# Hybrid decoder trunk on one core: low parts of 170 weight slabs kept in DRAM between the two halves of the tokens

## The chip, the core and the metric

The kernel runs on one core of a Trainium2 chip. The metric is the device time of one execution in microseconds (us); lower is better. The core has five engines that run their own in-order queues: PE (TensorE, matrix products; its weight loads are shown apart as PEld), DVE (VectorE), ACT (ScalarE), POOL (GpSimd) and SP (SyncE, which here only issues DMAs). DMAs issued by any of them are carried out by 16 DMA engines.

## The reference

A decoder of two layers over 1024 tokens of width 1024, all in float32. Each layer adds three things to the residual h: a mixer of four groups of heads, a cross-attention to 256 memory tokens, and a gated feed-forward of width 2816.

```python
for l in range(DEPTH):                       # DEPTH = 2
    proj = rms_norm(h, norm_mix[l]) @ w_in[l]
    ret_p, rw_p, ssm_p, dsa_p = split_cols(proj, GROUP_COLS)
    ...                                      # retention, RWKV-7, Mamba-2, sparse attention
    h = h + concat([o_ret, o_rw, o_ssm, o_dsa]) @ w_out[l]
    h = h + cross_attention(rms_norm(h, norm_cross[l]), memn, wq, wk, wv, wo)
    h = h + conv_glu(rms_norm(h, norm_ffn[l]), w_up, conv_w, conv_b, w_down)
return rms_norm(h, norm_final)
```

## The kernel before

Everything is held feature-major, and the tokens are worked through in two halves of 512 (`hf` 0 and 1). A large product keeps the accuracy of float32 by splitting both operands into a high part that PE's faster format holds exactly and a low part, the rest. `mm3` (L263) then issues three products for each 128 x 128 block of weights: high by high, high by low, and low by high.

Weights come in **slabs**: 128 partitions by up to 1024 columns, 512 KB. `slab` (L268) makes one. It takes a raw buffer (`wraw`, three of them in pool `wr`), queues its load on SP (L272), copies the high part on ACT into one of two `whi` buffers (L254) and subtracts on DVE for the low part into one of two `wlo` buffers (L258). The raw buffer is free again when the subtraction has read it; `whi` and `wlo` are free when the slab's products are done. A slab of 1024 columns has 24 products of 512 tokens. In the two passes of the out-projection slabs have 640 and 384 columns (15 and 9 products), in the last product of the feed-forward 512 or 640.

The same slab is needed once for each half of the tokens, and before the change it is loaded, copied and subtracted anew each time: 644 slabs in all.

The stages of the main work follow one another in the order that `schedule` (L1829) writes out: the in-projection `proj` (P, 27 slabs a half) and what comes behind the mixers, `outer` (O, 124 slabs a half: out-projection, cross-attention, feed-forward; 8 of them are keys and values, and the last O loads 8 slabs twice). With (layer, half) in brackets and the start of each stage's slabs in the trace:

- P(0,0) from 0 us, together with the first keys and values of the memory tokens
- P(0,1) from about 200 us, beside the rest of the memory tokens
- O(0,0) from about 520 us
- P(1,0) from about 1240 us
- O(0,1) from about 1440 us
- P(1,1) from about 2085 us
- O(1,0) from about 2260 us
- O(1,1) from about 2960 us to the end at 3517.8 us

Beside the main work run two chains of mixer steps (`left`, `right`): many small operations on DVE and ACT with small products on PE, and many DMAs on SP. `paced` (L1790) deals their steps out among those of the main work. A scheduler then orders the instructions of each engine by priority and by its own estimate of when each can run; `urgent` (L391) sets the slabs' steps ahead. Each engine then runs its queue in that order. By about 960 us, 1900 us and 2560 us most of the mixer work of a half is done.

```python
    def mm3(self, out, wh, wl, xh, xl, start=True, stop=True):
        self.mm(out, wh, xh, start, False)
        self.mm(out, wh, xl, False, False)
        self.mm(out, wl, xh, False, stop)
```

Of the kernel before, what the change touches and what calls it, by code (L numbers as in the profile page):

```python
# [9 lines left out]
F32 = mybir.dt.float32  # L10
# [21 lines left out]
MP = 8 * 16 * 129  # words from one 128 x 128 matrix to the next, so that diagonal blocks lie evenly  # L32

# ---------------------------------------------------------------- host layout
GROUPS = [4, 4, 4, 5, 5]
MO_ORDER = [2, 3, 6, 7, 4, 5, 0, 1]  # tiles of the mixers' outputs as they are used
MO_SPLIT = 5
# how far ahead of their place in the program the steps go that the main products wait for
URGENT = 3000
# steps of the in-projection of the first half before the norm of the memory tokens; products of the memory tokens ahead  # L40
# of the in-projection of the second half
PRE, AHEAD = 7, 2
RATE = 100, 100  # of the two chains of mixers against the main work
# [31 lines left out]
J = {"rw": 0, "ds": 8, "rt": 12, "ss": 16}  # first tiles of the in-projection's parts  # L75
# [18 lines left out]
def _consts():  # L94
# [33 lines left out]
    # within a chunk of 64: s < t, s <= t twice, and behind the diagonal blocks of 16  # L128
# [86 lines left out]
# ---------------------------------------------------------------- device  # L215
# head e of a pair, chunk c; partitions of the head's features, of the chunk, and of the chunk where those of e = 1
# have changed places
# [3 lines left out]
class Slab:  # L221
    """hi and lo parts, indexed as one [128, 2, ...] tile"""
# [8 lines left out]
class K:  # L231
    def __init__(self, ctx, tc, a, out, dbg=None):
# [7 lines left out]
        self.wr = pool("wr", 3)  # L240
        self.ws = pool("ws", 2)
# [9 lines left out]
    # ---- helpers  # L251
    def hilo(self, hi, lo, src, lo_eng=None):
        """hi + lo == src exactly, both representable as float32r."""
        self.nc.scalar.copy(hi, src)  # L254
        self.lo(lo, src, hi, lo_eng)
# [12 lines left out]
    def slab(self, src, n=1024):  # L268
        with self.urgent():
            raw = self.wr.tile([128, 1024], F32, name="wraw", tag="wraw")  # L270
            with self.tc.issue_after(self.first.ins) if 0 < len(self.loads) < 4 else nullcontext():
                self.loads.append(self.nc.sync.dma_start(raw[:, :n], src))  # L272
            hi = self.ws.tile([128, 1024], F32R, name="whi", tag="whi")
            lo = self.ws.tile([128, 1024], F32R, name="wlo", tag="wlo")
            self.hilo(hi[:, :n], lo[:, :n], raw[:, :n])
        return Slab(hi, lo)

    def after(self, n):
        """Queues loads behind that of slab n."""
        return self.tc.issue_after(self.loads[n].ins)  # L280
# [4 lines left out]
    def bc(self, ap, n):  # L285
        """[P, 1] -> [P, n] with step 0."""
        return ap.to_broadcast([ap.shape[0], n])

    def rsq(self, pool, src, n, scale, eps, name, bufs=None):
        """(src * scale + eps) ** -0.5 for a [128, n] tile of a few columns."""  # L290
# [10 lines left out]
    # ---- constants  # L301
    def setup(self):
# [11 lines left out]
        # the tables of ScalarE are loaded before the first data are there  # L314
# [40 lines left out]
    # ---- RMSNorm of a feature-major half: hi/lo tiles  # L355
    def sq_acc(self, acc, x, k, eng=None):
        """acc (+)= x * x for tile k of KC; the last addition is the one that is waited for"""
# [9 lines left out]
    def rstd(self, acc, n, nfeat, side=False):  # L367
        """(sum of acc over partitions / nfeat + eps) ** -0.5, token-major"""
# [7 lines left out]
    def rstd_bc(self, r, n):  # L376
        """r on every partition, tokens along the columns"""
# [5 lines left out]
    def gained(self, x, gname, l, k, dst=None):  # L383
        """hi/lo of x times the norm's gain; 1 / rms follows behind the product"""
# [9 lines left out]
    # ---- in-projection of one half  # L394
# [10 lines left out]
    def proj(self, l, hf):  # L405
# [26 lines left out]
        for item in order:  # L432
# [6 lines left out]
            for j in js:  # L439
                w = self.slab(self.a["win"][l, J[name] + j])  # L440
# [4 lines left out]
                # 1 / rms comes in behind the first products  # L445
# [21 lines left out]
    def proj_tok(self, l, hn, r, dst):  # L467
        pss = [(self.pa if t < 2 else self.pt).tile([128, 512], F32, name="ptok", tag="acc")
               for t in range(4)]
        for k0, kn in ((0, 3), (3, 3), (6, 2)):  # L470
            w = self.slab(self.a["wtok"][l, :, k0 * NTOK:(k0 + kn) * NTOK], kn * NTOK)
# [11 lines left out]
    # ---- keys and values of the memory tokens  # L483
# [54 lines left out]
    # ---- out-projection, cross-attention and ConvGLU of one half  # L538
# [9 lines left out]
    def dense(self, l, w, xs, hs, acc, norm):  # L548
        for ks in (range(MO_SPLIT), range(MO_SPLIT, KC)):
            for o in range(8):  # L550
                s = self.slab(self.a[w][l, o, :, ks[0] * 128:(ks[-1] + 1) * 128], len(ks) * 128)
# [43 lines left out]
    def cross(self, l, hn, acc, hs, gain):  # L595
# [9 lines left out]
        def query(h, i):  # L605
            s = self.slab(self.a["wq"][l, 2 * h + i])
# [62 lines left out]
        def out(hp, xo, os):  # L669
            for o in os:  # L670
                s = self.slab(self.a["wo2"][l, hp, o])
# [51 lines left out]
    def ffn(self, l, hf, hn, hs, acc, norm):  # L723
        nc = self.nc
        rb = None  # 1 / rms comes in behind the products
# [6 lines left out]
        def up(f):  # L732
            nonlocal rb
            pss = []
            for i in range(2):
                s = self.slab(self.a["wup"][l, 2 * f + i])
# [37 lines left out]
        for gi, g in enumerate(groups):  # L774
# [11 lines left out]
            # at the very end by halves of the tokens, so that the output of one is scaled beside the other's products  # L786
            parts = [slice(0, TH // 2), slice(TH // 2, TH)] if last and self.own else [slice(0, TH)]
            fin = iter(())
            for cs in parts:
                w = cs.stop - cs.start  # L790
                for o in range(0, 8, 2):
                    # the last tile's products come last in a pair
                    pair = []
                    for o2 in range(2):
                        s = self.slab(self.a["wdn"][l, o + o2, :, g[0] * 128:(g[0] + n) * 128], n * 128)
# [34 lines left out]
    # ---- RWKV-7: elementwise parts by quarters, then blocks of 128 tokens with two chunks of 64  # L830
# [39 lines left out]
    def rw_shift(self, dst, raw, l, hf, c0, tiles):  # L870
        """tiles of the projection with the mix of each token and the one before it"""
# [29 lines left out]
    def rw_pre(self, l, hf, qr, p):  # L901
# [20 lines left out]
        # k (1 + (a - 1) k_a) with a = (1 + ta) / 2  # L922
# [844 lines left out]
    def pool(self, name, bufs, side):  # L1767
        return self.tc.tile_pool(name=name, bufs=bufs, side=side, reuse_waits="tile")
# [96 lines left out]
```

## Time and profile before

| | |
|---|---|
| time, median of 3 runs | 3524.32 us (3523.21 to 3525.83) |
| profiled execution, first to last instruction (span) | 3517.8 us |
| busy: PE, PEld, DVE, ACT, POOL | 96%, 79%, 73%, 49%, 12% of the span |
| low-part subtractions on DVE (L258) | 644, 668.4 us |
| high-part copies on ACT (L254) | 644, 566.9 us |
| moved by DMA | 460.84 MB, mean 131 GB/s |

The profile gives the span of the profiled execution and no other time of its own; the median of the runs lies 6.5 us above it. Products overlap in PE's pipeline, so that one is shown with 0.39 us where the next follows 0.227 us later; PE counts as idle only where no product is under way.

### The profile page before, as it was taken

The page shows a single profiled execution, that of the slowest core. Times are in us where ns is not written, and L with a number is a line of the kernel's source. Part 1 is how long each engine was busy: PE and PEld are TensorE (multiplying, and loading weights), DVE is VectorE, ACT ScalarE, POOL GpSimd, SP SyncE. Part 2 cuts the span into 40 slices and gives each one's busy share as a digit, 9 for nine tenths or more (in the row PEclk, how much of TensorE's full clock was granted, in tenths as well). Part 3 has the DMA queues.
Part 4 walks back from the last instruction along what each step waited for, and adds up shares of the span by engine and source line. Part 5 has one row for each costly group of instructions (what it writes and reads, how often), then busy time and mean ns, then how long its engine had stood idle before and what let it go on. Part 6 is the DMA issues. An engine that isn't in the chain of part 4 may idle for free.

```text
span 3517.8 us, 55280 instructions
## 1 busy us (share of the span) xinstructions
PE 3375.9 (96%) x20256; PEld 2769.4 (79%) x20256; DVE 2578.5 (73%) x5225; ACT 1732.3 (49%) x3298; POOL 412.8 (12%) x449
## 2 busy tenths in 40 slices
PE   8999998999899999999999999999899999999998
PEld 6788886777688877777888887777688888788887
DVE  5885778898879877976886555787888776565555
ACT  4454654588346543544643343378446543443333
POOL 1100002110111111000211010010111112111001
PEclk9999999999999999999999999999999999999999
DMA  8665456432233356433243336532243334222233
GB/s 267 207 196 159 142 195 193 133 98 86 82 112 93 104 193 223 149 110 102 92 130 102 107 120 204 191 116 77 78 130 98 112 102 153 88 93 91 96 102 114
DMA packets 318920, 460.84 MB, mean 131 GB/s; under 512 B 75192, under 2 KB 200504, under 8 KB 318648
## 3 DMA queue, kind: packets, MB, share of 16 engines
q1 hardware_dynamic: 279592, 400.93, 36.1%
q10 hardware_dynamic: 39056, 56.38, 4.6%
q8 instruction: 159, 2.61, 0.3%
q14 instruction: 113, 0.93, 0.1%
HBM read 377.96 MB, written 79.23 MB: 130 GB/s over the span
## 4 chain that ended last, share of the span: by engine, by line
PE 67%; DVE 14%; DMA 7%; ACT 6%; issue 5%; SPq 1%; POOL 0%; ACTq 0%; DVEq 0%; POOLq 0%
PE pacc L261 54%; DVE wlo L258 3%; ACT d_P L1654 3%; DMA d_P<-ds 2%; DVE hn L388 1%; DVE d_P L1630 1%; ACT whi L254 1%; PE dov L261 1%; DVE h L542 1%; PE lg L261 1%; PE dlg L261 1%; PE dtp L1731 1%; PE po L261 1%; DMA d_Q<-in_tab_dram 1%; DMA r_N<-nd 1%
## 5 line engine op out<-in xcount | busy, mean ns | idle before, releaser
L261 PE MATMUL pacc<-hn,whi 128*128 128x512 f32 x5376 | 1725.0, 399 | 31.8 <-ACT hn L254 8.5
L261 PEld LDWEIGHTS pacc<-hn,whi 128*128 128x128 f32 x5376 | 1011.3, 190 | 254.4 <-DVE hn L388 13.2
L261 PE MATMUL pacc<-hn,wlo 128*128 128x512 f32 x2688 | 1071.3, 399 | 33.8 <-DVE wlo L258 33.2
L254 ACT CAST whi<-wraw 128x1024 fp32r<-128x1024 f32 (+5 forms) x644 | 566.9, 882 | 748.5 <-PE pacc L261 591.9
L258 DVE TENSOR_TENSOR wlo<-wraw,whi 128x1024 fp32r<-128x1024 f32 (+5 forms) x644 | 668.4, 1039 | 99.3 <-ACT whi L254 79.0
L261 PE MATMUL pacc<-act,whi 128*128 128x512 f32 (+1 forms) x2256 | 659.4, 375 | 5.1 <-ACT whi L254 4.1
L261 PEld LDWEIGHTS pacc<-hn,wlo 128*128 128x128 f32 x2688 | 511.3, 190 | 155.5 <-DVE wlo L258 49.6
L261 PEld LDWEIGHTS pacc<-act,whi 128*128 128x128 f32 x2256 | 408.5, 189 | 81.1 <-ACT whi L254 8.9
L261 PE MATMUL pacc<-act,wlo 128*128 128x512 f32 (+1 forms) x1128 | 421.6, 377 | 6.8 <-DVE wlo L258 6.5
L542 DVE TENSOR_TENSOR h<-pacc,h 128x512 f32<-128x512 f32 (+1 forms) x296 | 198.1, 672 | 167.6 <-PE pacc L261 166.6
L1654 ACT ACTIVATE d_P<-d_SC,d_cand 128x384 bf16<-128x384 f32 (+3 forms) x248 | 219.1, 884 | 81.1 <-DVE d_cand L1649 66.8
L261 PEld LDWEIGHTS pacc<-act,wlo 128*128 128x128 f32 x1128 | 213.1, 189 | 47.7 <-DVE wlo L258 11.0
L365 POOL TENSOR_TENSOR acc<-acc,sq 128x512 f32<-128x512 f32 (+1 forms) x78 | 107.9, 1383 | 607.5 <-ACT sq L364 601.0
L766 POOL TENSOR_TENSOR cv<-cv,acc 128x512 f32<-128x512 f32 x88 | 125.7, 1429 | 101.4 <-ACT th L765 101.2
L1630 DVE TENSOR_SCALAR_CACHE_REDUCE d_P<-d_SC,d_cand 128x512 bf16<-128x512 f32 (+4 forms) x144 | 135.7, 942 | 2.6
L767 DVE SCALAR_TENSOR_TENSOR cv<-th,cv 128x512 f32<-128x512 f32 x88 | 60.4, 687 | 86.9 <-POOL cv L766 86.9
L765 ACT ACTIVATE th<-cv 128x512 f32<-128x512 f32 x88 | 55.5, 631 | 122.2 <-DVE cv L762 121.7
L254 ACT CAST act<-cv 128x512 fp32r<-128x512 f32 x88 | 54.6, 621 | 121.3 <-DVE cv L769 117.7
L754 DVE TENSOR_TENSOR gs<-pacc,acc 128x512 f32<-128x512 f32 x88 | 60.5, 688 | 71.4 <-PE pacc L261 68.4
L421 DVE TENSOR_TENSOR pev<-pacc,rb 128x512 f32<-128x512 f32 x96 | 65.4, 685 | 42.5 <-PE pacc L261 39.3
L388 DVE SCALAR_TENSOR_TENSOR hn<-h,vec,hn 128x512 fp32r<-128x512 f32 x96 | 90.8, 952 | 3.9 <-ACT hn L387 3.5
L387 ACT ACTIVATE hn<-h,vec 128x512 fp32r<-128x512 f32 x96 | 68.4, 720 | 50.9 <-DVE h L542 49.1
(392 smaller groups left out, 4584.0 us busy)
## 6 DMA issues: line engine op xcount, KB each, us to landing
wraw<-in_wup_dram SPq DMA_DIRECT2D x176, 512.0 KB, 3.3
wraw<-in_win_dram SPq DMA_DIRECT2D x96, 512.0 KB, 3.9
wraw<-in_wdn_dram SPq DMA_DIRECT2D x96, 256.0 KB, 2.6
wraw<-in_wdn_dram SPq DMA_DIRECT2D x72, 320.0 KB, 2.9
wraw<-in_wq_dram SPq DMA_DIRECT2D x32, 512.0 KB, 3.3
wraw<-in_wo_dram SPq DMA_DIRECT2D x32, 512.0 KB, 3.2
r_IN<-sp SPq DMA_DIRECT2D x32, 320.0 KB, 3.8
wraw<-in_wout_dram SPq DMA_DIRECT2D x32, 320.0 KB, 2.7
```

What stands on the lines that cost most here:

```text
L254: self.nc.scalar.copy(hi, src)
L258: (eng or self.nc.vector).tensor_tensor(out=lo, in0=src, in1=hi.bitcast(F32), op=OP.subtract)
L261: self.nc.tensor.matmul(out, lhsT=lhsT, rhs=rhs, start=start, stop=stop)
L365: (eng or (nc.vector if k == KC - 1 else nc.gpsimd)).tensor_tensor(out=acc, in0=acc, in1=s[:, :n], op=OP.add)
L387: self.nc.scalar.mul(hl[:, 0, :], x, g)
L388: self.nc.vector.scalar_tensor_tensor(hl[:, 1, :], x, g, hl[:, 0, :].bitcast(F32), op0=OP.mult, op1=OP.subtract)
L421: nc.vector.tensor_tensor(out=e, in0=ps, in1=rb, op=OP.mult)
L542: self.nc.vector.tensor_tensor(out=h, in0=ps, in1=h, op=OP.add)
L754: nc.vector.tensor_tensor(out=gs[:, 2:], in0=pss[0], in1=rb, op=OP.mult)
L766: nc.gpsimd.tensor_tensor(out=c, in0=c, in1=rb, op=OP.mult)
L1630: ts(junk[:, :n], SC[big[i]], c, None, op0=op, op1=OP.add, accum_out=dst[:, i:i + 1])
L1654: nc.scalar.activation(junka[:, :n], SC[big[i]], AF.Sign, bias=c, accum_out=cnt[:, i:i + 1])
```

## The change

- Of each half-0 slab of the in-projection of both layers (27 + 27) and of `outer` of layer 0 (116: not the keys and values) the low part is also stored to DRAM after the subtraction, by a DMA on SP outside of `urgent`.
- When half 1 comes to the same slab, the raw weights are loaded and the high part copied as before, but the low part is loaded from DRAM by a second DMA on SP. DVE has no subtraction for it. That is 170 slabs: those of P(0,1), O(0,1) and P(1,1).
- `wraw` goes from three buffers to two, `wlo` from two to three, `whi` keeps two; the memory taken is the same.
- `outer` of layer 1 and the slabs of the memory tokens, keys and values do as before, with the new number of buffers.

The diff, without the lines that only take comments away:

```diff
-        self.wr = pool("wr", 3)
-        self.ws = pool("ws", 2)
+        self.wr = pool("wr", 2)
+        self.ws = pool("ws", 3)
+        self.kept = {}
...
-    def slab(self, src, n=1024):
+    def slab(self, src, n=1024, key=None):
+        nc = self.nc
         with self.urgent():
             raw = self.wr.tile([128, 1024], F32, name="wraw", tag="wraw")
+            hi = self.ws.tile([128, 1024], F32R, name="whi", tag="whi", bufs=2)
+            lo = self.ws.tile([128, 1024], F32R, name="wlo", tag="wlo", bufs=3)
             with self.tc.issue_after(self.first.ins) if 0 < len(self.loads) < 4 else nullcontext():
-                self.loads.append(self.nc.sync.dma_start(raw[:, :n], src))
-            hi = self.ws.tile([128, 1024], F32R, name="whi", tag="whi")
-            lo = self.ws.tile([128, 1024], F32R, name="wlo", tag="wlo")
-            self.hilo(hi[:, :n], lo[:, :n], raw[:, :n])
+                self.loads.append(nc.sync.dma_start(raw[:, :n], src))
+            nc.scalar.copy(hi[:, :n], raw[:, :n])
+            if key in self.kept:
+                nc.sync.dma_start(lo[:, :n].bitcast(F32), self.kept[key])
+            else:
+                self.lo(lo[:, :n], raw[:, :n], hi[:, :n])
+        if key is not None and key not in self.kept:
+            self.kept[key] = self.dram("_".join(map(str, ("lo",) + key)), [128, n])
+            nc.sync.dma_start(self.kept[key], lo[:, :n].bitcast(F32))
         return Slab(hi, lo)

+    def key(self, l, *at):
+        return (l,) + at if self.keep[at[0]] > l else None
...
-                w = self.slab(self.a["win"][l, J[name] + j])
+                w = self.slab(self.a["win"][l, J[name] + j], key=self.key(l, "in", J[name] + j))
...
-                s = self.slab(self.a["wup"][l, 2 * f + i])
+                s = self.slab(self.a["wup"][l, 2 * f + i], key=self.key(l, "out", "up", 2 * f + i))
...
+        self.keep = {"in": 2, "out": 1}
```

The other calls of `slab` in `proj_tok`, `dense`, `cross` and `ffn` get their keys in the same way.

## Rows read from the trace of the kernel before

**Rows 1.** The page: span, and PE's busy time, share and instructions.

```profile
span 3517.8 us, 55280 instructions
PE 3375.9 (96%) x20256; PEld 2769.4 (79%) x20256; DVE 2578.5 (73%) x5225; ACT 1732.3 (49%) x3298; POOL 412.8 (12%) x449
```

**Rows 2.** The page: shares of the chain that ended last, by engine.

```profile
PE 67%; DVE 14%; DMA 7%; ACT 6%; issue 5%; SPq 1%; POOL 0%; ACTq 0%; DVEq 0%; POOLq 0%
```

**Rows 3.** The chain in order of time (start, us): its longest piece, in O(1,1).

```profile
3152.51 320.78 PE pacc L261 x1415
```

**Rows 4.** Stretch, length; busy PE, PEld, DVE, ACT, POOL; granted clock, DMA share, GB/s.

```profile
0.00:200.00 200.00, 183.98 (x929) 149.66 (x930) 145.10 (x341) 97.46 (x190) 31.09 (x41) 0.99 0.69 228
200.00:520.00 320.00, 313.49 (x2746) 268.24 (x2744) 228.34 (x569) 157.95 (x338) 7.29 (x15) 0.99 0.55 173
520.00:960.00 440.00, 399.49 (x2707) 314.08 (x2708) 376.45 (x787) 273.50 (x544) 62.06 (x56) 0.97 0.39 119
1240.00:1440.00 200.00, 191.55 (x984) 157.12 (x983) 152.97 (x354) 92.24 (x187) 25.29 (x32) 0.99 0.59 194
1440.00:2085.00 645.00, 626.77 (x3884) 510.59 (x3883) 459.39 (x941) 295.61 (x577) 72.19 (x77) 0.99 0.36 111
2085.00:2260.00 175.00, 171.56 (x843) 139.91 (x842) 107.63 (x193) 65.34 (x114) 22.12 (x17) 1.00 0.56 186
2260.00:2560.00 300.00, 269.99 (x2109) 210.38 (x2108) 244.39 (x539) 200.25 (x403) 26.26 (x24) 0.94 0.34 107
```

**Rows 5.** Groups by line and shape: copies and subtractions (busy us, mean ns, idle before).

```profile
L258 DVE TENSOR_TENSOR wlo<-wraw,whi 128x1024 fp32r<-128x1024 f32 x368 | 457.3, 1243 | 76.0 <-ACT whi L254 56.6 <-PE rbc L261 16.9 <-PE dtp L1731 0.3
L254 ACT CAST whi<-wraw 128x1024 fp32r<-128x1024 f32 x368 | 385.5, 1048 | 449.7 <-PE pacc L261 336.3 <-issue 56.9 <-PE lg L261 11.6
L258 DVE TENSOR_TENSOR wlo<-wraw,whi 128x512 fp32r<-128x512 f32 x128 | 88.4, 691 | 10.9 <-ACT whi L254 10.8
L258 DVE TENSOR_TENSOR wlo<-wraw,whi 128x640 fp32r<-128x640 f32 x104 | 87.7, 846 | 9.4 <-ACT whi L254 8.8
L258 DVE TENSOR_TENSOR wlo<-wraw,whi 128x384 fp32r<-128x384 f32 x32 | 21.5, 671 | 0.0
```

**Rows 6.** Waits of PE (us, times, longest) in 200 to 520, P(0,1).

```profile
PE pacc L261 <- DVE wlo L258: 0.7, 1, 0.7
```

**Rows 7.** Waits of PE in 1440 to 2085 us, O(0,1).

```profile
PE g L261 <- DVE r_Z L1057: 4.2, 1, 4.2
...
PE pacc L261 <- DVE wlo L258: 2.6, 3, 1.2
```

**Rows 8.** Waits of PE in 2085 to 2260 us, P(1,1).

```profile
PE pacc L261 <- DVE wlo L258: 2.1, 1, 2.1
```

**Rows 9.** Waits of PE in 520 to 960 us, O(0,0).

```profile
PE pacc L261 <- DVE wlo L258: 15.2, 15, 2.6
```

**Rows 10.** Waits of PE in 2260 to 2560 us, O(1,0).

```profile
PE pacc L261 <- DVE wlo L258: 10.5, 5, 5.9
```

**Rows 11.** Waits of SP's queue, whole span.

```profile
SPq L272 <- DVE wlo L258: 1588.9, 417, 14.8
```

**Rows 12.** DMA issues: KB each, median us to landing.

```profile
wraw<-in_wup_dram SPq DMA_DIRECT2D x176, 512.0 KB, 3.3
...
sp<-r_o SPq DMA_DIRECT2D x16, 512.0 KB, 3.9
...
wraw<-in_wout_dram SPq DMA_DIRECT2D x32, 192.0 KB, 2.5
```

**Rows 13.** Busy time by stretch, five us of P(0,0), columns as in rows 4.

```profile
80.00:85.00 5.00, 5.00 (x35) 5.00 (x34) 0.92 (x2) 2.19 (x4) 1.06 (x1) 1.00 1.05 400
```

**Rows 14.** ACT in order of time (start, us), slabs of 384 columns in O(1,1).

```profile
2995.56 0.52 ACT L254 CAST whi<-wraw 128x384 fp32r<-128x384 f32 x1 [2.88 <-PE pacc L261]
...
2999.70 0.50 ACT L254 CAST whi<-wraw 128x384 fp32r<-128x384 f32 x1
```

**Rows 15.** DVE in order of time, the subtraction of the first of these.

```profile
2996.39 0.55 DVE L258 TENSOR_TENSOR wlo<-wraw,whi 128x384 fp32r<-128x384 f32 x1
```

More of the change, by code (lines that the diff above doesn't have):

```diff
@@ L470, in proj_tok @@
         for k0, kn in ((0, 3), (3, 3), (6, 2)):
-            w = self.slab(self.a["wtok"][l, :, k0 * NTOK:(k0 + kn) * NTOK], kn * NTOK)
+            w = self.slab(self.a["wtok"][l, :, k0 * NTOK:(k0 + kn) * NTOK], kn * NTOK, self.key(l, "in", "tok", k0))
             for t in range(4):
@@ L550, in dense @@
             for o in range(8):
-                s = self.slab(self.a[w][l, o, :, ks[0] * 128:(ks[-1] + 1) * 128], len(ks) * 128)
+                s = self.slab(self.a[w][l, o, :, ks[0] * 128:(ks[-1] + 1) * 128], len(ks) * 128, self.key(l, "out", o, ks[0]))
                 ps = self.pa.tile([128, TH], F32, name="pacc", tag="acc")
@@ L605, in query @@
         def query(h, i):
-            s = self.slab(self.a["wq"][l, 2 * h + i])
+            s = self.slab(self.a["wq"][l, 2 * h + i], key=self.key(l, "out", "q", 2 * h + i))
             ps = self.pa.tile([128, TH], F32, name="pacc", tag="acc")
@@ L670, in out @@
             for o in os:
-                s = self.slab(self.a["wo2"][l, hp, o])
+                s = self.slab(self.a["wo2"][l, hp, o], key=self.key(l, "out", "o", hp, o))
                 for o2 in range(2):
@@ L794, in ffn @@
                     for o2 in range(2):
-                        s = self.slab(self.a["wdn"][l, o + o2, :, g[0] * 128:(g[0] + n) * 128], n * 128)
+                        s = self.slab(self.a["wdn"][l, o + o2, :, g[0] * 128:(g[0] + n) * 128], n * 128,
+                                      self.key(l, "out", "dn", o + o2, g[0]))
                         ps = self.pa.tile([128, TH], F32, name="pacc", tag="acc")[:, :w]
```

## The prediction

> **What bounds the kernel now.** I read the page's busy times first, then the chain, then the stretches of each stage, then who makes PE wait in them. PE is busy for 3375.9 of 3517.8 us, so 142 us are all that can come back without taking products away [rows 1]. The chain agrees: two thirds of it are PE, 14% DVE [rows 2]. How fast PE goes when nothing holds it up is seen in the last stage, where 1415 products follow one another in 320.78 us, 0.227 us each [rows 3]; a slab of 24 products then takes 5.44 us, one of nine 2.04 us. No matter how the low parts are made, this part of the time stays.
>
> The idle time is spread unevenly [rows 4]. Stretch length less PE's busy time gives 16.0 us in P(0,0), 6.5 in P(0,1), 40.5 in O(0,0) up to 960 us, 8.5 in P(1,0), 18.2 in O(0,1), 3.4 in P(1,1) and 30.0 in the first 300 us of O(1,0). The change lifts subtractions off DVE in P(0,1), O(0,1) and P(1,1) only. These hold 6.5 + 18.2 + 3.4 = 28.1 us of idle time. The two stretches where DVE is fullest and PE waits most, O(0,0) with 376 of 440 us of DVE and O(1,0) with 244 of 300, keep every subtraction. So the first reading is: a large saving on DVE, in the wrong places for most of PE's waits.
>
> **The change part by part.** *Subtractions removed.* A slab of 1024 columns costs DVE 1.243 us, one of 640 0.846, of 512 0.691, of 384 0.671 [rows 5]. Each half of an in-projection has 27 slabs, taken at 1.243 all: 33.6 us, twice 67. `outer` of layer 0 has 60 of 1024 columns (74.6 us), 8 + 16 of 640 (20.3), 24 of 512 (16.6) and 8 of 384 (5.4), together 116.9. DVE loses 184 us of work in three stretches where it has 228 + 459 + 108 = 795 us [rows 4], 23%. Almost all of that lies beside PE's products and is worth nothing by itself.
>
> What of it is on the path: PE's waits for a low part in these stretches, 0.7 us [rows 6], 2.6 [rows 7] and 2.1 [rows 8], in all **5.4 us**, of which I count all as won, because the load of the low part can be asked for three slabs ahead (see below). For the other 28.1 - 5.4 = 22.7 us DVE is a helper: the longest of these waits in O(0,1) is one of 4.2 us for a mixer's operation on DVE [rows 7]. The bounds are nothing and 22.7. With 23% less in its queue and not all of the waits being DVE's I take a third, **7.6 us**. The clock also counts: in P(0,1) and O(0,1) the granted clock averages 0.99 [rows 4], so 0.01 x (320 + 645) = 9.7 us of full speed are lost there, PE having fallen to its lower level (1.2 instead of 2.4 GHz) around waits. If 13 of 28 us of idle time go, the same share of that goes: **4.5 us** (bounds 0 and 9.7). Gain 17.5 us, at most 28.1 + 9.7 = 38.
>
> *A third raw buffer less.* This holds for all 644 slabs, the 474 that still subtract above all. Now the load of a slab waits for the subtraction three slabs before it, afterwards for the one two before (after a stored low part, for the copy). For slabs of 1024 columns there is room: two slabs are 10.9 us, and copy 1.05, subtraction 1.24 [rows 5] and load 3.3 us [rows 12] take 5.6, so DVE may be 5.3 us late. For 384 columns there is none: in the calm O(1,1) the subtraction that belongs to the copy at 2995.56 ends at 2996.39 + 0.55 = 2996.94 [rows 14, 15]; plus 2.5 us of load [rows 12] that is 2999.44, and the copy two slabs on starts at 2999.70 [rows 14]. Of 32 such slabs 8 take their low part from DRAM. If the other 24 lose a quarter of a microsecond each that is **6 us**, my value, since the calm stretch shows them just in time and two of the four halves are not calm. The lower end is 0, since the high parts' two buffers hold the copy back anyway. For the upper end see the slow rival: 37 us.
>
> *The wait on SP.* SP is already held at the head of its queue by raw loads waiting for subtractions, 1588.9 us in all [rows 11]. A store waits for the subtraction of its own slab, the event that the raw load next to it waits for too; a low-part load waits until the products of the slab three before are done, shortly before the raw load behind it becomes possible. What is queued behind are the mixers' loads and stores; they meet the same events as now. I cost it at nothing; if SP's order puts a mixer's load behind a low-part load by mistake, it is late by up to a slab, 5.4 us, each time. The low part itself has two slabs of time, 10.9 us, for a load of 3.3 us, so it isn't late; for 512 columns it still has 5.4 us.
>
> *Transfers.* Stored are 13.9 MB for each in-projection (24 slabs of 0.524 MB, 1.3 MB for the rest) and 47.2 MB in `outer`, 75 MB, and as much is loaded: 461 MB become 611. Nothing in the trace stores a low part; the nearest row is a store of 512 KB, 3.9 us to landing [rows 12]. In P(0,0) 13.9 MB more in 200 us are 70 GB/s on top of 228; with the busy share growing alike, 0.69 becomes 0.90; P(1,0) goes from 0.59 to 0.80, O(0,1) from 0.36 to 0.60 [rows 4]. The engines do fill for short times in P(0,0), 1.05 at 400 GB/s [rows 13], so a 512 KB store ahead of a raw load delays it by 0.524 MB / 400 GB/s = 1.3 us. The 5.3 us above cover it. Bounds: 0, and 27 x 1.3 = 35 us if every one were exposed; I take **1 us**, as the room is four times the delay.
>
> Sum: -5.4 - 7.6 - 4.5 + 6 + 1 = -10.5 us on the span of 3517.8, 3507.3. The 6.5 us between span and median stay: 3524.3 - 10.5 = **3513.8 us**.
>
> **The rivals.** *No effect.* The DVE time was idle time to begin with; only the 5.4 us of direct waits come back and the 6 + 1 us of buffers and transfers eat them. For it: in O(0,1) all but 18 of 645 us of PE are busy, after 1900 us nearly all. Against it: the 4.2 us wait of a mixer. It gives 3524, at most 7 us either way.
>
> *Slower: two raw buffers are too few where DVE is crowded.* In O(0,0) and O(1,0) DVE works through mixer steps in order, the subtraction stands behind them, and PE already waits 15.2 and 10.5 us for low parts [rows 9, 10]. With two raw buffers a late subtraction delays the next load but one and so itself again. It decides from the point where DVE is more than 5.3 us late for a wide slab, 0.3 us for a narrow one. If these waits double, that is 26 us more, and the clock lost there, 0.03 x 440 + 0.06 x 300 = 31 us [rows 4] for 70.5 us of idle time, grows by 11. With the 37 us and the 17.5 us of gain: 3524 + 37 - 17.5 = 3544. Against it: the room of 5.3 us for most slabs.
>
> *Much faster: PE has more room than its busy time shows.* In P(0,1) PE loads weights for 268.2 of 320 us, 84%, in O(0,1) 510.6 of 645, 79%, in P(1,1) 139.9 of 175, 80% [rows 4]. If less work on DVE let the latter two reach 84%, they would take 609 and 167 us, 44 us less: 3480. The Trainium skill, "Perfetto Trace Analysis", Identifying the Most-Contended Engine, says this is the number to go by: the share of time in weight loads and not the busy time of the products, which is pipelined. Against it: mixer products are small and of other shapes, with weight loads of another length, so the share can differ with no idle time at all.
>
> *The keys never match*, and nothing is loaded: then DVE keeps its 2578 us and all pay for two raw buffers. The names in the diff are the same in both halves; I leave it no chance.
>
> **How the numbers follow.** Forecast 0.52 (3500 to 3520), no effect 0.20, slower 0.22, much faster 0.06. About 0.2%, 7 us, is what a measurement of this kernel can tell from no change: 3517.3 to 3531.4. Of the forecast 0.07 lies within it. Faster 0.45 + 0.06 = 0.51, same 0.07 + 0.20 = 0.27, slower 0.22. The range goes from full gain at no cost, 3524 - 38 = 3486, to just past the slow rival, 3546; outside are the much faster case and half of the slow one, 0.17.
>
> **What would show it.** Right: 474 subtractions instead of 644, DVE about 184 us less busy; PE's waits for low parts gone in P(0,1), O(0,1) and P(1,1); waits for high parts (whose data are then late) up by no more than 6 us; O(0,1) shorter, O(0,0) and O(1,0) as long as before. Wrong: O(0,0) or O(1,0) longer with PE waiting for high or low parts there (the slow rival); DMA shares at 1 in P(0,0) or P(1,0) with PE waiting on loads; or another order of the mixers on PE, which the scheduler may choose since its own estimate of DVE has changed. That last is in no row and could move any stage by some microseconds.

## The result, and the profile after

| | before | after |
|---|---|---|
| median of the runs, us | 3525.07 (3523.21 to 3526.91) | 3567.96 (3560.64 to 3571.49) |
| ratio, 95% interval | | 1.012, 1.0104 to 1.0136 |
| profiled execution, us | 3517.8 | 3569.4 |

The change costs 1.2%, 42 us, where 10.5 us of gain were forecast. The wrong side, and outside the range. Because the runs below were timed at different moments, each beside its own runs of before, they are compared here by their ratio: "+42" is 0.012 x 3524 us.

The page of after answers to [rows 1] and [rows 2] (span; busy times with share and instructions; chain by engine):

```profile
span 3569.4 us, 55531 instructions
PE 3398.9 (95%) x20256; PEld 2787.7 (78%) x20256; DVE 2423.6 (68%) x5055; ACT 1729.7 (48%) x3298; POOL 401.6 (11%) x449
PE 66%; DVE 13%; DMA 10%; ACT 6%; issue 3%; SPq 1%; POOL 0%; ACTq 0%; POOLq 0%; DVEq 0%
```

DVE did lose 170 instructions and 154.9 us of busy time. (The durations of the subtractions taken away add up to 184 us; DVE's instructions overlap at their ends, and busy time counts an overlap once.) PE, with the same 20256 products, is idle for 3569.4 - 3398.9 = 170.5 us instead of 141.9 (+28.6) and busy for 23.0 us more: the mean granted clock fell from 0.986 to 0.977. In the chain one share has grown: DMA, from 7% to 10%.

The stretches of [rows 4], with the same lengths, laid where each stage now lies (columns as there):

```profile
0.00:200.00 200.00, 181.07 (x895) 148.42 (x896) 140.04 (x307) 89.34 (x173) 29.42 (x41) 0.97 0.88 293
209.00:529.00 320.00, 303.44 (x2658) 259.15 (x2657) 200.19 (x550) 156.01 (x337) 8.37 (x14) 0.97 0.66 207
539.00:979.00 440.00, 392.37 (x2770) 305.44 (x2768) 367.86 (x777) 267.65 (x538) 57.54 (x57) 0.95 0.55 170
1277.00:1477.00 200.00, 193.05 (x971) 159.11 (x969) 139.27 (x313) 82.14 (x164) 29.02 (x33) 0.98 0.82 275
1472.00:2117.00 645.00, 629.73 (x3899) 515.46 (x3900) 365.22 (x855) 302.15 (x594) 70.87 (x77) 0.98 0.57 183
2115.00:2290.00 175.00, 168.70 (x825) 137.77 (x824) 72.89 (x156) 60.68 (x106) 19.77 (x16) 0.99 0.82 270
2295.00:2595.00 300.00, 268.37 (x2054) 206.69 (x2053) 241.83 (x525) 197.38 (x397) 26.92 (x22) 0.93 0.32 99
```

In O(0,1) DVE is busy for 365.2 of 645 us instead of 459.4, and PE is idle for 15.3 us instead of 18.2: relieving DVE there bought next to nothing. In P(0,1) PE lost 10 us of its 320 although DVE has 28 us less to do. In every stage with stores or loads the DMA share has gone up, in P(0,0) from 0.69 to 0.88 and in P(1,0) from 0.59 to 0.82.

Where the time goes is best seen from the start of the same slab's high-part copy on ACT, which carries the same number in both kernels (644 of them). Each figure is how much later the first slab of a stage starts than in the profiled execution of before, in us:

```
                   P(0,1)  O(0,0)  P(1,0)  O(0,1)  P(1,1)  O(1,0)  O(1,1)   end
after               +5.1   +15.9   +44.8   +31.3   +30.6   +33.8   +43.0   +51.7
```

The loss is made in P(0,0) (+5.1), P(0,1) (+10.8) and above all in O(0,0) (+28.9), where 116 stores were added and nothing was taken away. The stages that were to gain, O(0,1) and P(1,1), stand still or lose (-0.7 and +3.2). P(1,0) gives 13.5 back, O(1,0) and O(1,1) cost 9.2 and 8.7. These figures hold a new order of the mixers' steps too; runs below take it out.

Who makes PE wait, whole span (us, times, longest), answering to [rows 6 to 10]; first after, then two rows of before:

```profile
PE pacc L262 <- DVE wlo L259: 34.9, 39, 3.1
PE pacc L262 <- ACT whi L279: 21.8, 23, 3.2
...
PE pacc L262 <- DMA wlo<-lo_in: 1.3, 1, 1.3
```

```profile
PE pacc L261 <- DVE wlo L258: 39.7, 40, 5.9
PE pacc L261 <- ACT whi L254: 9.3, 17, 1.8
```

The direct waits for low parts made on DVE fell only from 39.7 to 34.9, and waits for high parts, that is for raw data, rose by 12.5. The loaded low parts are nearly always in time. SP's queue, answering to [rows 11] (L278 issues the raw loads, L281 those of the low parts):

```profile
SPq L278 <- DVE wlo L259: 1122.8, 300, 12.7
SPq L281 <- PE pacc L262: 327.9, 110, 7.6
```

The transfers themselves (KB each, median us to landing), first after, then before, beside [rows 12]:

```profile
wraw<-in_win_dram SPq DMA_DIRECT2D x96, 512.0 KB, 5.6
lo_in<-wlo SPq DMA_DIRECT2D x48, 512.0 KB, 6.5
wlo<-lo_in SPq DMA_DIRECT2D x48, 512.0 KB, 4.1
d_P<-ds SPq DMA_DIRECT2D x24, 256.0 KB, 6.8
```

```profile
wraw<-in_win_dram SPq DMA_DIRECT2D x96, 512.0 KB, 3.9
d_P<-ds SPq DMA_DIRECT2D x24, 256.0 KB, 4.3
```

Transfers that the change doesn't touch land later: the in-projection's raw slabs after 5.6 instead of 3.9 us, a mixer's `d_P` after 6.8 instead of 4.3. The second isn't owed to the added transfers alone: in buf_only, below, which adds none but has another order, `d_P` lands after 6.0 us (the in-projection's raw slabs after 3.6). A store of a low part takes 6.5 us, not the 3.9 of the row that it was costed by. What late transfers do is seen in the chain that ended last (start, us, what). Among its 195 longest pieces 49 are DMA, 34 before. Those of after in P(1,1):

```profile
2150.64 3.87 DMA ds<-pev
2155.22 9.28 DMA d_P<-ds
2169.71 5.71 DMA r_raw<-rw
2185.11 4.95 DMA wlo<-lo_in_tok
2193.82 4.27 DMA d_P<-ds
2218.39 7.21 DMA r_raw<-rw
2226.37 3.97 DMA rw<-pev
2241.59 4.31 DMA d_Q<-iqd
```

and those of before in the same stage:

```profile
2150.18 6.18 DMA d_Q<-in_tab_dram
2160.69 5.22 DMA d_P<-ds
```

One of the eight is a load of a low part; the others are the mixers' own stores and loads.

### The profile page after: what moved, and what is told of

It is laid out like the page before. It is cut to its first block, busy times and chain, and to the rows that moved or that the text cites. A ratio compares the mean times of both kernels' runs of the same rounds, so it can differ in the third digit from the quotient of the medians.

```text
span 3569.4 us, 55531 instructions
## 1 busy us (share of the span) xinstructions
PE 3398.9 (95%) x20256; PEld 2787.7 (78%) x20256; DVE 2423.6 (68%) x5055; ACT 1729.7 (48%) x3298; POOL 401.6 (11%) x449
## 4 chain that ended last, share of the span: by engine, by line
PE 66%; DVE 13%; DMA 10%; ACT 6%; issue 3%; SPq 1%; POOL 0%; ACTq 0%; POOLq 0%; DVEq 0%
PE pacc L262 53%; ACT d_P L1669 3%; DVE wlo L259 2%; DMA d_P<-ds 2%; ACT whi L279 1%; DVE hn L402 1%; PE po L262 1%; DMA nt<-mo 1%; PE dov L262 1%; PE dlg L262 1%; DVE h L556 1%; PE lg L262 1%; DMA r_raw<-rw 1%; PE dtp L1746 1%; DVE d_P L1645 1%
## 5 line engine op out<-in xcount | busy, mean ns | idle before, releaser
L259 DVE TENSOR_TENSOR wlo<-wraw,whi 128x1024 fp32r<-128x1024 f32 (+4 forms) x474 | 484.7, 1023 | 100.9 <-ACT whi L279 90.4
L402 DVE SCALAR_TENSOR_TENSOR hn<-h,vec,hn 128x512 fp32r<-128x512 f32 x96 | 83.0, 870 | 16.1 <-ACT hn L401 15.8
```

What stands on the lines that cost most here:

```text
L259: (eng or self.nc.vector).tensor_tensor(out=lo, in0=src, in1=hi.bitcast(F32), op=OP.subtract)
L402: self.nc.vector.scalar_tensor_tensor(hl[:, 1, :], x, g, hl[:, 0, :].bitcast(F32), op0=OP.mult, op1=OP.subtract)
```

## The experiments

The runs set three causes against each other: the buffers (2 raw, 3 low), the transfers, and the order into which the scheduler puts the rest once it counts on other durations. Times are medians; +us are by ratio as above, with the 95% interval of the ratio.

### The buffers alone, and the change without them

**buf_only**: the change's buffers, nothing stored or loaded.

```diff
-        self.keep = {"in": 2, "out": 1}
+        self.keep = {"in": 0, "out": 0}
```

> Two raw, two high and three low buffers, and nothing is stored or loaded: all 644 low parts are subtracted as before. Computes the same. Buffer theory (the loss comes from asking for raw slabs two instead of three ahead): nearly the whole loss, 3555 to 3570 us, with O(0,0) longer by 20 us or more. Transfer theory (the loss comes from the 150 MB more on the DMA engines): only what the changed kernel lost where it neither stores nor loads, 9 us in O(1,0) and 8 us in the last pass of O(1,1), so 3535 to 3545, and O(0,0) as long as before within 8 us.

Measured 3529.46, ratio 1.0028 (1.0018 to 1.0037): **+10 us**, less than either theory had asked for. The scheduler made a new order here too, so the price of the buffers includes that.

**three_raw**: the change with the buffers of before.

```diff
-        self.wr = pool("wr", 2)
+        self.wr = pool("wr", 3)
-            lo = self.ws.tile([128, 1024], F32R, name="wlo", tag="wlo", bufs=3)
+            lo = self.ws.tile([128, 1024], F32R, name="wlo", tag="wlo", bufs=2)
```

> The change with the buffers of before, three raw and two low: stores and loads stay. Buffer theory: 3515 to 3528, the loss is gone and what the freed DVE time is worth shows. Transfer theory: the last stages come back, O(0,0) stays longer by some 25 us, 3545 to 3555.

Measured 3564.85, 1.0126 (1.0108 to 1.0144): **+44 us**, no better than after. This is above what either theory expected. Giving the third raw buffer back doesn't mend the change. Its price is the third low one: here PE waits for loaded low parts, 31.1 us in all, most of it in the in-projections.

```profile
PE pacc L262 <- DMA wlo<-lo_in: 14.4, 11, 3.6
PE pacc L262 <- DMA wlo<-lo_out_dn: 5.6, 4, 2.1
PE pacc L262 <- DMA wlo<-lo_out_up: 4.1, 4, 1.4
PE ptok L262 <- DMA wlo<-lo_in_tok: 3.8, 2, 2.9
PE pacc L262 <- DMA wlo<-lo_out: 2.9, 4, 1.3
```

### One half of the change at a time

**stores_only**: three_raw, the 170 stores made, but every slab subtracted again in the second half.

```diff
-            if key in self.kept:
+            if False:
```

> Buffers of before. The 170 low parts are stored in the first half of the tokens, but the second half subtracts again and loads nothing: 75 MB more are moved, DVE is spared nothing. Computes the same. Buffer theory: 3520 to 3530. Transfer theory: the loss of P(0,0) and O(0,0) with no gain anywhere, 3545 to 3565.

Measured 3540.74, 1.0051 (1.0034 to 1.0068): **+18 us**, between the two.

**loads_only**: three_raw, one low part stored; all 170 loads read that one table (the products of the second half then use its numbers).

```diff
-            self.kept[key] = self.dram("_".join(map(str, ("lo",) + key)), [128, n])
-            nc.sync.dma_start(self.kept[key], lo[:, :n].bitcast(F32))
+            if not self.kept:
+                self.one = self.dram("lo_one", [128, 1024])
+                nc.sync.dma_start(self.one, lo.bitcast(F32))
+            self.kept[key] = self.one[:, :n]
```

> Buffers of before. Only one low part is ever stored; each of the 170 slabs of the second half loads its low part from that one place, so all but one of them multiply with another slab's low part (the output is not the reference's). 75 MB of loads and 184 us less on DVE in P(0,1), O(0,1), P(1,1), no stores. If freed DVE time is worth what I forecast (17 us): 3508 to 3515. If it is worth nothing, as the unchanged length of O(0,1) in the changed kernel suggests: 3520 to 3530. If loads hurt P(0,1): up to 3535.

Measured 3540.02, 1.0055 (1.0040 to 1.0070): **+19 us**, above all three expectations. Each half costs, and the two sum to the +44 of three_raw within their intervals. But in all of these the scheduler made a new order, so part of each figure may be luck of the order.

### In one order

Each of the next kernels is built twice: first with the transfers left out, to read off the order of the instructions on the five engines that the scheduler gives before (for loads: with the subtractions in the places that they have there), then with the transfers added and every engine held to that order.

**freed_same_order**: no subtraction for the 170 slabs of the second half and no transfer; the products take the high part in the place of the low one.

```diff
-                nc.sync.dma_start(lo[:, :n].bitcast(F32), self.kept[key])
+                lo = hi
```

> Buffers and order of before, nothing stored or loaded; for the 170 slabs of the second half there is no subtraction, and the high part stands in for the low one (the output is not the reference's). It prices the freed 184 us of DVE by themselves. My forecast had 17.5 us for it: 3500 to 3508. If the DVE time was idle time to begin with: 3514 to 3522.

Measured 3515.37, 0.9977 (0.9968 to 0.9986): **-8 us**. This is all that the relief of DVE can give in this order, with transfers for nothing.

**stores_same_order**, **loads_same_order** and **both_same_order** are stores_only, loads_only and three_raw in the order of before.

> As stores_only (buffers of before, 170 stores, nothing loaded, all 644 subtractions), but every engine issues what the kernel before had in exactly the order of the kernel before; the scheduler only places the stores between the others on SP. Transfer theory (the DMA engines and SP's queue are what costs): 3535 to 3545, as stores_only. Order theory (the scheduler, seeing other times in its estimate, deals out the mixers' steps in another order, and that order stalls PE more): 3518 to 3526.

Measured 3556.56, 1.0097 (1.0082 to 1.0113): **+34 us**.

> As loads_only (buffers of before, one low part stored, 170 loaded from there, so the output is not the reference's), with the order of the kernel before on every engine, less the 170 subtractions. Transfer theory: 3530 to 3545. Order theory: 3510 to 3526, the waits for late low-part loads (29.6 us in loads_only, where two low buffers let the load start only when the slab two before is done) being the rest.

Measured 3574.81, 1.0155 (1.0138 to 1.0172): **+55 us**, 63 more than freed_same_order. PE waits for loads, a row that neither before nor after has:

```profile
PE pacc L263 <- DMA wlo<-lo_one: 38.6, 25, 4.9
```

> As three_raw (the change with three raw and two low buffers), with the order of the kernel before on every engine, less the 170 subtractions. Transfer theory: 3555 to 3570, as three_raw. Order theory: 3515 to 3530.

Measured 3606.84, 1.0243 (1.0226 to 1.0261): **+86 us**, about the sum 34 + 55. All three lie above both of their ranges. So a new order isn't what makes the change slow. On the contrary, with the same buffers the scheduler's own order has only half of the loss (+44).

### What of a store costs

Both keep stores_same_order instruction for instruction.

**stores_8_columns**: each store takes 8 columns.

```diff
-                nc.sync.dma_start(self.kept[key], lo[:, :n].bitcast(F32))
+                nc.sync.dma_start(self.kept[key][:, :8], lo[:, :8].bitcast(F32))
```

> As stores_same_order, instruction for instruction in the same order on every engine, SP included, and with the same waits, but each of the 170 stores carries 8 columns instead of up to 1024: 0.7 MB instead of 75. If the bytes on the DMA engines cost the 32 us: 3518 to 3530. If a store that waits at the head of SP's queue for its subtraction, or the low part's buffer that has to wait for a store, costs them: 3545 to 3558.

Measured 3533.12, 1.0031 (1.0018 to 1.0044): **+11 us**.

**stores_of_a_constant**: from a table of constants, up to 896 columns (66 MB in all), so that no store waits for a subtraction or holds a low buffer.

```diff
-                nc.sync.dma_start(self.kept[key], lo[:, :n].bitcast(F32))
+                n = min(n, 896)
+                nc.sync.dma_start(self.kept[key][:, :n], self.cm.rearrange("p a b -> p (a b)")[:, :n])
```

> The counterpart: the same places in SP's queue, but each store (all but the first two) takes its up to 896 columns from a table that is there from the start, so it waits for no subtraction and no low-part buffer waits for it; 66 MB are still moved. What lands in DRAM isn't used. If the bytes cost: 3548 to 3558. If the waits cost: 3518 to 3530.

Measured 3551.6, 1.0085 (1.0068 to 1.0103): **+30 us**. The waits and the held buffers gone, bytes kept: nearly all of the 34 remains. The bytes gone, waits kept: a third remains. A store costs mostly by its bytes on the DMA engines, which delay what else is under way there: in stores_same_order `d_P` lands after 7.0 us, with 8 columns after 5.7, before after 4.3.

```profile
d_P<-ds SPq DMA_DIRECT2D x24, 256.0 KB, 7.0
```

```profile
d_P<-ds SPq DMA_DIRECT2D x24, 256.0 KB, 5.7
```

The two figures, 30 without waits and 11 without bytes, add up to more than 34; with intervals of 5 to 6 us either way it can't be told whether they overlap. By slab starts, as in the table above, stores_same_order loses 11.1 us in P(0,0), 12.4 in O(0,0) and 9.0 in P(1,0), where the stores are, and 5 in all the rest. PE is idle for 27 us more than before; some 12 of them are longer waits for high and low parts, the rest are waits of the mixers' products and other small ones.

### What of a load costs

**loads_nobody_reads**: freed_same_order, and each low part is loaded in full into its buffer, but the products take the high part.

```diff
+                nc.sync.dma_start(lo[:, :n].bitcast(F32), self.kept[key])
                 lo = hi
```

> As freed_same_order (no subtraction in the second half, the high part stands in for the low one, so the output is not the reference's), but each of the 170 slabs also loads a low part of full size that nothing reads: the bytes and the places on SP are there, and no product waits for them. freed_same_order took 3515, loads_same_order 3575. If the bytes cost: 3555 to 3575. If the products' wait for loads that start late costs (two low buffers): 3515 to 3530.

Measured 3580.78, 1.0163 (1.0146 to 1.0180): **+57 us**. This run can't be read as the price of the bytes. Nothing tied the loads to their slabs, so 96 of the 170 stand within 220 us of O(0,1), and SP's queue waits for loads of its own:

```profile
SPq L281 <- DMA wlo<-lo_one: 128.9, 84, 4.0
```

There a mixer's load stood behind them, and PE waited 23.2 us for it at a stretch:

```profile
PE mp L263 <- DMA r_y<-yd: 23.5, 2, 23.2
```

The next three therefore keep every load at its place in loads_same_order, with the high part read in the place of the low one. **loads_in_place_unread** loads in full; **loads_to_dram_in_place** loads into a DRAM table for each slab, so that no load waits for a buffer; **loads_8_columns_in_place** loads 8 columns.

```diff
                 dst, m = lo[:, :n].bitcast(F32), n
+                dst = self.dram("_".join(map(str, ("cp",) + key)), [128, n])  # loads_to_dram_in_place
+                dst, m = lo[:, :8].bitcast(F32), 8                            # loads_8_columns_in_place
                 nc.sync.dma_start(dst, self.kept[key][:, :m])
+                lo = hi                                                       # all three
```

> Every instruction stands where it stands in loads_same_order: 170 low parts are loaded in full (75.9 MB) on SP's queue at the same places, but the products take the high part in the place of the low one (so this is no longer the reference's result), and nothing waits for a low part's landing; a load waits only for the load that was in its buffer before. Against 3574.8 of loads_same_order and 3515.4 without transfers. Theory A, the bytes take up the DMA engines and the other transfers land later: at least 3550. Theory B, the products' waits for the low parts and the waits of SP's queue for the products make the loss: under 3530.

Measured 3538.79, 1.0037 (1.0022 to 1.0051): +13 us, **21 more than freed_same_order**.

> As loads_in_place_unread, same places on SP's queue, but each load goes to a DRAM table of its own, so that no load waits for anything and nothing waits for it: the bytes alone, with no wait behind them on SP's queue. The products take the high part in the place of the low one. Theory A (bytes): within 10 us of loads_in_place_unread. Theory B (a queue that is held by its waits): 3515 to 3525, as without transfers.

Measured 3535.02, 1.0028 (1.0015 to 1.0041): +10 us, **18 more**.

> As loads_in_place_unread, same places and same waits on SP's queue, but each load brings 8 columns (4 KB) in the place of up to 1024: the instructions without the bytes. The products take the high part in the place of the low one. Theory A (bytes): 3515 to 3530. Theory B (the instructions and their waits on SP's queue): at the time of loads_in_place_unread.

Measured 3515.94, 0.9982 (0.9971 to 0.9994): -6 us, **2 more**, which is nothing that can be told apart.

Neither theory was right alone: A had asked for at least 3550 from the first of the three, B for less than 3530. The instruction and its wait on SP cost nothing; the bytes cost about 20 us whether or not the queue waits; and the rest of the 63, some 42 us, is there only when the products read what is loaded: the 38.6 us of waits above and what follows from them. By slab starts the loads' bytes cost where DMA was fullest already: against freed_same_order loads_in_place_unread loses 8.1 us in P(0,1), 16.5 in P(1,1) and -0.5 in O(0,1) (loads_to_dram_in_place 10.5, 18.3 and 1.3).

How bytes that nobody waits for reach PE is plainest in P(1,1), columns as in [rows 4]; first freed_same_order, then loads_in_place_unread, then PE's two longest waits there:

```profile
2090.00:2258.00 168.00, 167.55 (x827) 137.02 (x827) 76.27 (x165) 61.97 (x109) 15.92 (x14) 1.00 0.58 187
2093.00:2277.00 184.00, 173.45 (x825) 140.90 (x824) 76.17 (x164) 61.74 (x108) 15.93 (x14) 0.96 0.74 246
PE isc L263 <- DMA d_Q<-iqd: 4.7, 1, 4.7
PE isc L263 <- DMA bg<-r_bg: 4.1, 1, 4.1
```

Without the loads PE is idle for 0.5 us there, with them for 10.6, nearly all of it in two waits for transfers of the mixers; and its products take 5.9 us longer, at a granted clock of 0.96 instead of 1.00.

### The third low buffer

The order of before can't be kept with two raw buffers, so these three have the change's buffers (2 raw, 3 low) and the order of buf_only; else they are stores, loads and both as above.

> As stores_same_order (170 stores, every slab subtracted, no load), but with the buffers and the order of buf_only: 2 raw and 3 low buffers. A store holds its low part's buffer until it has landed, so a third low buffer helps if that is what costs: then under 3529.5 + 20. If it is the bytes on the DMA engines: 3529.5 + 32, within 6 us.

Measured 3569.25, 1.0120 (1.0096 to 1.0144): +42 us, **32 more than buf_only**, as with two low buffers (34). That speaks against the buffer that a store holds, within intervals of 8 and 5 us either way.

> The buffers of the change (2 raw, 2 high, 3 low) and, on every engine, the order that the kernel with these buffers alone has (buf_only, 3529.5); one low part is stored and 170 loads bring it, as in loads_same_order. If the products wait for the loads because a load is only asked for when the products two slabs before are done, the third low buffer takes nearly all of these waits away: under 5 us of PE's time instead of 38.6, and the time is buf_only less 9 for DVE plus 20 for the bytes, 3535 to 3545. If the waits have another cause (the transfer itself, SP's queue), they stay near 38 us and the time is 3570 to 3585.

Measured 3546.14, 1.0054 (1.0039 to 1.0069): +19 us, **9 more than buf_only**. PE's waits for low and high parts:

```profile
PE pacc L263 <- DVE wlo L285: 29.9, 33, 3.0
PE pacc L263 <- ACT whi L279: 17.0, 22, 3.6
```

No row of a load is left. (The order and the raw buffers differ from those of loads_same_order too, so the third low buffer isn't the only thing changed.) With two low buffers a load is asked for when the products two slabs before are done, and 3.9 us to landing leave little of the next slab's 5.44 us [rows 3]; with three it has one slab more. What remains is -8 for DVE and about 17 for the bytes.

> As loads_third_low_buffer, with 170 stores and each load from its own table: the change itself in the order of buf_only. By the terms so far: 3529.5 - 9 + 20 for the loads' bytes + 32 for the stores = 3572, within 8 us, about what the change has in the scheduler's own order (3568). If the stores' cost comes on top of waits for loads that stay: 3605 or more.

Measured 3585.97, 1.0164 (1.0141 to 1.0187): **+58 us**. This is above the 3572 expected, in part because before itself took 3520 beside buf_only and 3525 beside this run. By ratio the parts give 10 (buffers) + 32 (stores) + 9 (loads less relief) = 51, within the interval's 8 of 58. The change itself in its own order has +42, so the scheduler's new order gives back about 15.

### Another way to relieve DVE

**subtract_on_gpsimd**: three_raw's buffers, no transfers; the 170 subtractions of the second half go to GpSimd.

```diff
-                nc.sync.dma_start(lo[:, :n].bitcast(F32), self.kept[key])
+                self.lo(lo[:, :n], raw[:, :n], hi[:, :n], nc.gpsimd)
```

> A version without transfers: buffers of before, nothing stored or loaded, the 170 subtractions of the second half are made on GpSimd instead of DVE. Computes the same. DVE is freed as in the change; a GpSimd operation on 512 columns takes 1.4 us in the kernel before, so some 2.8 us for 1024. If the freed DVE time is worth its 9 us of freed_same_order and GpSimd is in time: 3510 to 3518. If its slower subtraction is late for the products, or the other order of the mixers costs: 3525 to 3545.

Measured 3574.8, 1.0148 (1.0132 to 1.0163): **+52 us**. A subtraction of 1024 columns takes 2.43 us there instead of 1.24, though PE waits only 9.6 us for it directly:

```profile
L259 POOL TENSOR_TENSOR wlo<-wraw,whi 128x1024 fp32r<-128x1024 f32 x108 | 262.2, 2429 | 483.8 <-ACT whi L279 422.5 <-PE sp L262 23.6 <-issue 13.3
```

```profile
PE pacc L262 <- POOL wlo L259: 9.6, 13, 2.0
```

The reason lies on DVE, which this version doesn't relieve: it is busy for 2563.9 us, against 2578.5 before and 2424.3 in freed_same_order. Some of DVE's other operations take longer when they meet a subtraction on GpSimd (start, us):

```profile
1861.36 2.40 POOL L259 TENSOR_TENSOR wlo<-wraw,whi 128x1024 fp32r<-128x1024 f32 x1
1861.44 2.87 DVE L780 SCALAR_TENSOR_TENSOR cv<-th,cv 128x512 f32<-128x512 f32 x1 [0.48 <-POOL cv L779]
1864.42 0.69 DVE L782 SCALAR_TENSOR_TENSOR cv<-cv,pacc 128x512 f32<-128x512 f32 x1
```

The second of these takes 0.69 us in before. In this run 16 of its 88 instances overlap a subtraction on GpSimd and take 2.42 us on average, the other 72 take 0.69. `gs<-pacc,acc`, which reads a product out of PSUM (where PE leaves its products), takes 0.69 us with and without such an overlap. DVE's durations outside the subtractions add up to 2362 us instead of 2203. So the gain that was to pay for this version isn't there; how the 52 us divide between that, the late subtractions and the new order wasn't measured.

No version that computes the same was found that beats before. With 8 us to win in the order of before and some 20 us for the bytes of the loads alone, keeping the low parts in DRAM doesn't pay there.

## Why the prediction was wrong, point by point

**What bounds the kernel: right.** The idle time of PE was small where DVE was to be relieved, and the time hidden there stayed hidden.

**Subtractions removed: right in count, too large in worth.** 644 became 474, and their time fell by 184 us as forecast. The row of [rows 5] for after shows an unchanged duration:

```profile
L259 DVE TENSOR_TENSOR wlo<-wraw,whi 128x1024 fp32r<-128x1024 f32 x260 | 322.6, 1241 | 70.0 <-ACT whi L279 60.8 <-DMA lo_out_dn<-wlo 3.9 <-PE pacc L262 1.9
```

The gain of 17.5 us measured 8 (freed_same_order, 5 to 11). PE's direct waits for low parts fell from 39.7 to 33.5 us there, and little else came back; the third of the other idle time and the share of the clock did not. The 4.2 us wait of a mixer [rows 7] on which that third rested is still there in freed_same_order, as 5.8 us:

```profile
PE g L263 <- DVE r_Z L1084: 5.8, 1, 5.8
```

**Two raw buffers: right in size.** 6 us forecast, 10 measured (6 to 13), the scheduler's new order included, so that the size came out right in part by luck. In place it was half right. O(1,1) is slower, but hardly at the slabs of 384 columns, whose eight take 20.5 us instead of 18.9: the last 16 slabs, of 640 columns, take 42.7 us from the copy of the first to that of the last instead of 35.0, in buf_only 42.1, with three raw buffers 34.5.

**Transfers: the step that failed.** They were costed at 1 us because "the 5.3 us above cover it", with a bound of 35. Measured, with the order held: the stores 32 to 34 us, and 30 where no store waits for anything; the bytes of the loads 18 to 21. The DMA shares had been worked out well (0.90, 0.80 and 0.60 forecast; 0.88, 0.82 and 0.57 in the stretches above), but the argument then looked only at the raw loads of wide slabs. Those have room, though not always enough: PE's waits for high parts rose by 12.5 us in after, of which the buffers alone make 3.6 (12.9 us in buf_only). The mixers' transfers have none where each step of a chain waits for the one before (the two waits in P(1,1) of loads_in_place_unread, and the eight pieces of the chain there in after). The bound of 27 delayed raw loads counted P(0,0) alone and left out the mixers' transfers, the 116 stores in O(0,0) and all loads. The store was also costed at the 3.9 us of another store; it took 6.5. The loss of clock that follows waits (the last section) was in the sum as a gain of 4.5 us.

**The wait on SP: half right.** Cost at nothing is what loads_8_columns_in_place shows for the loads (+2). The stores' instructions without their bytes cost 11 us: a wait at the head of SP's queue, or the low buffer that a store holds. These two weren't taken apart, but a third low buffer left the price of the stores as it was. "The low part itself isn't late" is right with three low buffers (1.3 + 0.8 us of waits in after) and wrong with two (38.6).

**The rivals.** The slower one named a time, 3544, on the right side, but a wrong mechanism: PE's waits for low parts in the crowded stages were to double, and measured in O(0,0) and O(1,0)

```profile
PE pacc L262 <- DVE wlo L259: 15.5, 10, 3.1
...
PE pacc L262 <- DVE wlo L259: 6.5, 6, 2.7
```

against 15.2 [rows 9] and 10.5 [rows 10]. The much faster rival fell with freed_same_order: with the whole of the relief and none of the cost, 0.23% came back, not 44 us. The share of time in weight loads, which the Trainium skill, "Perfetto Trace Analysis", Identifying the Most-Contended Engine, names beside the share of peak arithmetic (MFU) as the measure to use instead of the products' busy time, stayed at 515.46 of 645 us in O(0,1) in after, 80%. It differs with no idle time to win, as was held against this rival: where PE is never idle, in the 320.78 us of [rows 3], it is 83% (265.6 us), and in P(1,1) of freed_same_order, with 0.5 us of idle time, 82%. That P(0,1) had 84% did not mean that O(0,1) could.

**The order of the mixers** was named as what "is in no row". It moved the time by about 15 us, in the change's favour.

## What to carry to other kernels

Work taken off an engine was worth here little more than the waits that ended on it in that very stage (8 us, 5.4 of them direct waits); read those first, and count the other idle time at nothing until a run shows otherwise. Bytes added to the DMA engines were paid for here by the transfers that were under way beside them, even where nothing waited for the added ones: look for the chains of small transfers (a store, a load, a step, a store) in the stages whose DMA share rises, and count the stages where a transfer is added as well as those where work is saved. To trade a subtraction of 1.24 us on an engine that isn't the bound for two transfers of 512 KB was a bad trade here, with DMA shares of 0.55 to 0.88 in the stages concerned.

## What was not expected of the hardware

A store and a load of equal bytes didn't cost alike: 75 MB of stores cost 32 to 34 us, as many bytes of loads 18 to 21. The traces don't say whether that is the direction or the stages in which they lie (the stores are in P(0,0), O(0,0) and P(1,0), the loads in P(0,1), O(0,1) and P(1,1)).

Part of the loss is clock. In after PE's busy time for the same products rose by 23.0 us of the 51.7, and its granted clock averaged 0.93 in the stretch 2295 to 2595 us, where before had 0.94 [rows 4], 0.95 in O(0,0) instead of 0.97, and 0.97 in P(0,0) and P(0,1) instead of 0.99. The clock has two levels, 2.4 and 1.2 GHz; the stretches granted at the lower one lasted 101.5 us in before and 165.8 in after, and PE had waited just ahead of each of them. So a wait for a transfer can be paid for a second time. How large that second part is differs: PE's busy time rose by 10.7 us of 37.6 in stores_same_order and by 13.8 of 52.5 in loads_same_order.
